# HGRN2 level products in blocks of 32 keys on four column tiles

## The chip, the cores and the metric

The kernel runs on one core of a Trainium2 chip. The metric is device time in microseconds of one execution, as the median over runs. The engines are named as in the profile: PE is TensorE's matmul and PEld its weight load, DVE is VectorE, ACT is ScalarE, POOL is GpSimd, SP is SyncE. L979 is line 979 of the kernel before.

## The reference

A hybrid decoder layer on 2048 tokens of width 1024 in float32. After an RMSNorm and one input projection, four HGRN2 heads of width 128 and eight RWKV-7 heads of width 64 run side by side. Their outputs go through an output projection and a ConvFFN. The change touches the HGRN2 heads alone, and in them the attention-like product within a chunk:

```python
b = jnp.cumsum(gb, axis=2)
diff = b[:, :, :, None, :] - b[:, :, None, :, :]
dec = jnp.exp(jnp.where(causal, diff, -jnp.inf))
A = jnp.einsum('bhtk,bhsk,bhtsk->bhts', qb, kb, dec)
o = jnp.einsum('bhts,bhsv->bhtv', A, vb) + jnp.einsum('bhtk,bhkv->bhtv', qb * jnp.exp(b), S)
```

Here gb is log f, and the decay from key s to query t is the product of f over the tokens between them. The state S is carried from chunk to chunk.

## The kernel before

The work has two stages. The first makes the projections, both kinds of heads and most of the output projection; the second is the ConvFFN. In the first stage three generators run in turn: `rw_stream` (RWKV, one unit for four heads on 512 tokens), `hg_stream` (HGRN, one unit for one head on 512 tokens, 16 units in all) and `dense` (projection matmuls, 128x512 each, three for one product of float32 operands that were split into a high and a low part). A round takes one step of `rw_stream` and one of `hg_stream`, and then `fill` adds dense work for 2000 ns of a written cost (`TICK`). This gives the order in which instructions are written; a list scheduler may move an instruction ahead of another on its engine. Each engine then runs its own list in order. Projection products go to the PSUM pair `pj`, RWKV's to `rw`, HGRN's to `hg`, which has two banks.

In `hg_unit` a head's 512 tokens stand along the free dimension, in four blocks of 128, and the 128 channels on the partitions. The decayed product of q and k in a block is built from levels. At the level of m tokens (m = 1, 2, 4, ..., 64), tokens are paired in runs of m. `scaled(l)` makes a tile X that holds k, scaled with the decay up to the end of its run, in each even run, and q, scaled with the decay from the start of its run, in each odd one. The product of the keys of an even run with the queries of the following odd run is then right for that pair of runs. `scaled` also carries the running products Pf and Sf to the next level, on DVE.

`level(lp, off, kt, qt, l)` makes the products of a level for all four blocks (L979). Up to the level of 32 tokens, blocks of 64 keys are used: for each of the eight blocks of 64 tokens, a weight load of 128 channels x 64 keys and a matmul of 32 queries (those of the odd runs), on the column tile at 0 or 64. The diagonal is one such product with all 64 queries and the unscaled q and k. The result stands with keys on PSUM partitions. `take(l, lp, off)` copies the wanted entries into the tile A (128 partitions, 4 blocks, 64 queries) with a predicated copy on DVE (L985), masked by a constant for the level. The diagonal is first written to A by a multiply with a mask (L997). The masks come with the constants, C_LV and C_DG, in the tile `cst`.

One step of the unit does the diagonal and levels 1, 2 and 4 (the diagonal in a bank of its own, l0, the levels in l1); three steps of `scaled` later another does levels 8, 16 and 32. Then ACT copies A into the two diagonal quarters of Af (128 keys x 128 queries a block). The level of 64 tokens follows as a product of 64x64 blocks (L1023) that ACT copies to the upper right quarter of Af. k scaled to the end of the block is transposed (L1021) and copied to KT by ACT, the states are made from it (L1032), and L1041 and L1042 give the output.

Of the kernel before, what the change touches and what calls it, by code (L numbers as in the profile page):

```python
# [7 lines left out]
F32 = mybir.dt.float32  # L8
F32R = mybir.dt.float32r
BF16 = mybir.dt.bfloat16  # L10
U32 = mybir.dt.uint32
AF = mybir.ActivationFunctionType
# [6 lines left out]
P = 128  # L19
# [10 lines left out]

C_CEN, C_ONE, C_S1, C_DG = 0, 128, 256, 384
C_LV = 448
C_SCAN = C_LV + 6 * 64
C_PAR = C_SCAN + 512
C_ID = C_PAR + 2
C_W = C_ID + 128
# [2 lines left out]
def make_consts():  # L39
    import numpy as np  # L40

    c = np.zeros((P, C_W), np.float32)
    p = np.arange(P)[:, None]
    q = np.arange(P)[None, :]
    same = ((p // 64) == (q // 64)).astype(np.float32)
    c[:, C_ID:C_ID + P] = p == q
    for f in range(2):
        c[:, C_PAR + f] = np.arange(P) % 2 == f
    c[:, C_CEN:C_CEN + P] = (p == q) - same / 64.0
    c[:, C_ONE:C_ONE + P] = same  # L50
    t = np.arange(64)[None, :]
    s = p % 64
    c[:, C_S1:C_S1 + 64] = t > s
    c[:, C_S1 + 64:C_S1 + 128] = t >= s
    c[:, C_DG:C_DG + 64] = t == s
    for l in range(6):
        m = 1 << l
        tq = np.arange(64).reshape(-1, 2, m)[:, 1, :].reshape(1, 32)
        c[:, C_LV + 64 * l:C_LV + 64 * l + 32] = ((tq // (2 * m)) == (s // (2 * m))) & ((s // m) % 2 == 0)
    c[:, C_SCAN:C_SCAN + 512] = (np.arange(512) % 64 != 0)[None, :]  # L60
    return c

# [2 lines left out]
def tile_layer(ctx, tc, consts, x, norm1_w, w_in, hg_lb_logits, hg_norm_w, rw_shift_mu, rw_w0, rw_w2,  # L65
# [4 lines left out]
    V, S, TE = nc.vector, nc.scalar, nc.tensor  # L70
# [13 lines left out]
    cst = cp.tile([P, C_ID], F32, name="cst")  # L84
# [5 lines left out]
    blk1 = cst[:, C_ONE:C_ONE + P]  # L90
    s1m = cst[:, C_S1:C_S1 + P]
    dgm = cst[:, C_DG:C_DG + 64]
    scanm = cst[:, C_SCAN:C_SCAN + 512]

    def pst(name):
# [14 lines left out]
    def act(out_, in_, func, **kw):  # L110

        want = tables.get(func)
        if want is not None and want != tab["now"]:
            pre = S.preload_act_table_set(want)
            for u_ in tab["uses"]:
                tc.add_manual_dep(pre.ins, u_.ins.name, NOSYNC, reason="table order")
            tab.update(now=want, pre=pre, uses=[])
        i_ = S.activation(out_, in_, func, **kw)  # L118
        if want is not None:
            tc.add_manual_dep(i_.ins, tab["pre"].ins.name, NOSYNC, reason="table order")  # L120
            tab["uses"].append(i_)
        return i_
# [12 lines left out]
    off = {}  # L135
    with tc.tile_pool(name="vp", bufs=1, reuse_waits="tile") as vp, tc.tile_pool(name="ps0", bufs=1, space=PSUM, reuse_waits="tile") as pools["ps"]:
        rows = vp.tile([P, P], F32, name="rows")
        V.memset(rows, 0.0)
        n = 0
# [127 lines left out]
    def phase1(c1):  # L267
# [3 lines left out]
        rp = c1.enter_context(tc.tile_pool(name="rp", bufs=1, reuse_waits="tile"))  # L271
# [11 lines left out]
        Af = hp.tile([P, 4, P], F32, name="Af")  # L283
# [6 lines left out]
        def bank(kind):  # L290
            return ps.tile([P, 512], F32, tag=kind, name=kind, bufs=2)
# [18 lines left out]
        def ev_lora(nb):  # L310
            def f(acc):
                t_ = stg("tl", "tl", 1)
                shift_mix(acc, 12, t_)
                act(t_[0:64, :], t_[0:64, :], AF.Tanh)
                stage[("tl", nb)] = t_
            return f
# [192 lines left out]
        def dense():  # L509
# [3 lines left out]
            for nb in range(NBLK):  # L513
                if nb >= 2:
                    jobs.append(("O", nb - 2))
                jobs.append(("A", nb))
                jobs.append(("P", 3584, ev_lora(nb), lambda nb=nb: done["rw1"] >= 2 * nb, None))
# [16 lines left out]

            at = [i for i, jb in enumerate(jobs) if jb[0] == "A"]
            extra = []
# [37 lines left out]
            for n, jb in enumerate(jobs):  # L574
                if jb[0] == "E":
                    jb[1]()
                    continue
                if jb[0] == "A":
                    if jb[1] == 0:
# [28 lines left out]
                acc = bank("pj")  # L608
                then = jobs[n + 1][1] if jobs[n + 1][0] == "A" else None
                for k in range(KD):  # L610
# [322 lines left out]
        def hg_unit(nb, j):  # L933
            q, f, v, gg = (stage.pop((n_, nb, j)) for n_ in "qfvg")
            k = rp.tile([P, BLK], F32, tag="hk", name="hk")
# [5 lines left out]
                TE.transpose(tp[:, b * P:(b + 1) * P], v[:, b * P:(b + 1) * P], ident)  # L941
            act(VT, tp.rearrange("p (b t) -> p b t", t=P), AF.Copy)
            yield
            A = rp.tile([P, 4, 64], F32, tag="hA", name="A")
            Pf = f
            Sf = rp.tile([P, BLK], F32, tag="Sf", name="Sf")
            V.memset(Sf.rearrange("p (n e) -> p n e", e=2)[:, :, 1:2], 1.0)
# [1 line left out]
            def scaled(l):  # L949

                m = 1 << l
                X = rp.tile([P, BLK], F32, tag="hX", name="hX", bufs=3)
                vw = lambda t_: t_.rearrange("p (n e m) -> p n e m", e=2, m=m)
                V.tensor_mul(vw(X)[:, :, 1, :], vw(q)[:, :, 1, :], vw(Pf)[:, :, 1, :])
                n_ = BLK // (2 * m)
                if l == 0:
                    act(vw(X)[:, :, 0, :], vw(k)[:, :, 0, :], AF.Copy)
                    act(vw(Sf)[:, :, 0, :], vw(Pf)[:, :, 1, :], AF.Copy)
                else:
                    V.tensor_mul(vw(X)[:, :, 0, :], vw(k)[:, :, 0, :], vw(Sf)[:, :, 0, :])  # L960
                    V.tensor_mul(vw(Sf)[:, :, 0, :], vw(Sf)[:, :, 0, :],
                                 vw(Pf)[:, :, 1, m - 1:m].broadcast_to([P, n_, m]))
                V.tensor_mul(vw(Pf)[:, :, 1, :], vw(Pf)[:, :, 1, :],
                             vw(Pf)[:, :, 0, m - 1:m].broadcast_to([P, n_, m]))
                return X

            def level(lp, off, kt, qt, l=None):

                w = 64 if l is None else 32
                for b in range(4):  # L970
                    for e in range(2):
                        t0 = (2 * b + e) * 64
                        qs = qt[:, t0:t0 + 64]
                        o = lp[e * 64:e * 64 + 64, off + b * w:off + b * w + w]
                        if l is not None:
                            m = 1 << l
                            qs = qs.rearrange("p (n e m) -> p n e m", e=2, m=m)[:, :, 1, :]
                            o = o.rearrange("p (n m) -> p n m", m=m)
                        TE.matmul(o, kt[:, t0:t0 + 64], qs, start=True, stop=True, tile_position=(0, e * 64))  # L979

            def take(l, lp, off):

                m = 1 << l
                mk = cst[:, C_LV + 64 * l:C_LV + 64 * l + 32].bitcast(U32).rearrange("p (n m) -> p n m", m=m)
                V.copy_predicated(A.rearrange("p b (n e m) -> p b n e m", e=2, m=m)[:, :, :, 1, :],  # L985
                                  mk.unsqueeze(1).broadcast_to([P, 4, 32 // m, m]),
                                  lp[:, off:off + 128].rearrange("p (b n m) -> p b n m", b=4, m=m))

            Xs = []
            for l in range(3):  # L990
                Xs.append(scaled(l))
                yield
            l0, l1 = bank("hg"), bank("hg")
            level(l0, 0, k, q)
            for l in range(3):
                level(l1, l * 128, Xs[l], Xs[l], l)
            V.tensor_mul(A, l0[:, 0:256].rearrange("p (b t) -> p b t", t=64), dgm.unsqueeze(1).broadcast_to([P, 4, 64]))  # L997
            for l in range(3):
                take(l, l1, l * 128)
            yield  # L1000
            Xs = []
            for l in range(3, 6):
                Xs.append(scaled(l))
                yield
            l1 = bank("hg")
            for l in range(3, 6):
                level(l1, (l - 3) * 128, Xs[l - 3], Xs[l - 3], l)
            for l in range(3, 6):
                take(l, l1, (l - 3) * 128)
            act(Af[0:64, :, 0:64], A[0:64], AF.Copy)  # L1010
            act(Af[64:128, :, 64:128], A[64:128], AF.Copy)
            yield
            X = scaled(6)
            V.tensor_mul(k, k, Sf)
# [4 lines left out]
            lp = bank("hg")  # L1019
            for b in range(4):  # L1020
                TE.transpose(tp[:, b * P:(b + 1) * P], k[:, b * P:(b + 1) * P], ident)  # L1021
            for b in range(4):
                TE.matmul(lp[0:64, b * 64:b * 64 + 64], X[:, b * P:b * P + 64], X[:, b * P + 64:b * P + 128],  # L1023
                          start=True, stop=True, tile_position=(0, 0))
# [44 lines left out]
        def hg_stream():  # L1069
            for n in range(4 * NBLK):  # L1070
                while ready["hg"] <= n:
                    yield None
                yield from hg_unit(n // 4, n % 4)
# [47 lines left out]
    with ExitStack() as c2:  # L1121
# [36 lines left out]
        with tc.tile_pool(name="op", bufs=1, reuse_waits="tile") as op_:  # L1158
# [7 lines left out]
            b = NBLK - 1  # L1166
# [41 lines left out]
            def weights(k, dh):  # L1208
                raw = ring("w", w_out[0, k * P:(k + 1) * P, dh * 512:dh * 512 + 512])
                wh, wl = (wo_[c].pop() if wo_[c] else  # L1210
                          op_.tile([P, 512], F32R, tag="wo" + c, name="wo" + c, bufs=3) for c in "hl")
                split_next(wh, wl, raw)
                return wh, wl
# [6 lines left out]
            for dh in range(2):  # L1220
                accs = [pst("wacc") for _ in range(4)]
                for n, k in enumerate((0, 1, 4, 5, 2, 3, 6, 7)):
                    w = weights(k, dh)
                    if dh == 0:
                        take(k)
                    if n == 5:
                        for i in range(4):
                            t0 = b * BLK + i * P
# [10 lines left out]
                    if dh == 1 and 2 <= n:  # L1239
                        for j in range(2):  # L1240
                            q = 2 * (n - 2) + j
# [3 lines left out]
                    for q in range(12):  # L1245
                        i, t_ = (q % 4, q // 4) if first else (q // 3, q % 3)
                        TE.matmul(accs[i], terms[t_][0][:, i * P:(i + 1) * P], terms[t_][1],
                                  start=n == 0 and t_ == 0, stop=n == KD - 1 and t_ == 2)
# [229 lines left out]
    with tc.tile_pool(name="dn", bufs=1, reuse_waits="tile") as dn:  # L1478
# [61 lines left out]
        for s_ in range(DS, N):  # L1540
            g, p, kk = steps[s_]
# [60 lines left out]
```

## Time and profile before

| | |
|---|---|
| median of three runs | 2675.3 us (2671.83 to 2676.13) |
| span of the profiled execution | 2678.7 us; the page gives no other time for it |
| instructions | 47929 |
| PE busy | 2595.9 us (97%) |
| DVE busy | 1964.4 us (73%) |
| ACT busy | 1368.4 us (51%) |
| POOL busy | 383.2 us (14%) |
| DMA | 510.54 MB, mean 191 GB/s |

An engine's busy time is the time in which at least one of its instructions was under way, so instructions that overlap count once; the mean ns of one is its own duration. Shapes of a matmul are given as rows*columns of the array that it uses, and then the partitions and elements of the moving operand. A row of waits reads: who waited, on what, for how many us in total, how often, and the longest.

### The profile page before, as it was taken

The page shows a single profiled execution, that of the slowest core. Times are in us where ns is not written, and L with a number is a line of the kernel's source. Part 1 is how long each engine was busy: PE and PEld are TensorE (multiplying, and loading weights), DVE is VectorE, ACT ScalarE, POOL GpSimd, SP SyncE. Part 2 cuts the span into 40 slices and gives each one's busy share as a digit, 9 for nine tenths or more (in the row PEclk, how much of TensorE's full clock was granted, in tenths as well). Part 3 has the DMA queues.
Part 4 walks back from the last instruction along what each step waited for, and adds up shares of the span by engine and source line. Part 5 has one row for each costly group of instructions (what it writes and reads, how often), then busy time and mean ns, then how long its engine had stood idle before and what let it go on. Part 6 is the DMA issues. An engine that isn't in the chain of part 4 may idle for free. (4 is left out here: it accounts for less than half of the span.)

```text
span 2678.7 us, 47929 instructions
## 1 busy us (share of the span) xinstructions
PE 2595.9 (97%) x18059; PEld 2089.1 (78%) x18059; DVE 1964.4 (73%) x3744; ACT 1368.4 (51%) x2200; POOL 383.2 (14%) x686
## 2 busy tenths in 40 slices
PE   7999999999999999999999999999999999999998
PEld 5877777777777777778778888887888888888887
DVE  4877767676567675667678789988998888676556
ACT  4556453554545455344457655456555545545444
POOL 6433222212222123222100000000000000000000
PEclk9999999999999999999999999999999999999999
DMA  8654443355643546844584458756754463898665
GB/s 301 202 164 165 163 142 116 115 162 183 201 152 115 153 157 221 277 131 129 172 287 139 138 188 262 239 172 194 260 199 150 149 203 124 318 322 280 204 193 185
DMA packets 312702, 510.54 MB, mean 191 GB/s; under 512 B 46879, under 2 KB 143509, under 8 KB 312469
## 3 DMA queue, kind: packets, MB, share of 16 engines
q1 hardware_dynamic: 257937, 329.13, 37.3%
q0 software_dynamic: 54464, 178.32, 20.4%
q8 instruction: 142, 2.33, 0.4%
q14 instruction: 91, 0.75, 0.1%
q10 hardware_dynamic: 68, 0.02, 0.0%
HBM read 373.13 MB, written 134.22 MB: 189 GB/s over the span
## 5 line engine op out<-in xcount | busy, mean ns | idle before, releaser
L263 PE MATMUL pj<-hh,wh 128*128 128x512 f32 x960 | 394.1, 411 | 6.7 <-ACT rkv L118 1.6
L264 PE MATMUL pj<-hl,wh 128*128 128x512 f32 x960 | 377.9, 394 | 0.0
L265 PE MATMUL pj<-hh,wl 128*128 128x512 f32 x960 | 377.7, 394 | 0.0
L263 PE MATMUL ua<-Bh,uwh 128*128 128x512 f32 x704 | 276.1, 392 | 3.8 <-ACT m L118 2.6
L265 PE MATMUL ua<-Bh,uwl 128*128 128x512 f32 x704 | 274.3, 390 | 0.0
L264 PE MATMUL ua<-Bl,uwh 128*128 128x512 f32 x704 | 274.1, 389 | 0.0
L263 PEld LDWEIGHTS pj<-hh,wh 128*128 128x128 f32 x960 | 181.1, 189 | 56.6 <-issue 9.1
L265 PEld LDWEIGHTS pj<-hh,wl 128*128 128x128 f32 x960 | 181.0, 189 | 39.6 <-issue 0.2
L264 PEld LDWEIGHTS pj<-hl,wh 128*128 128x128 f32 x960 | 181.3, 189 | 34.3 <-issue 0.6
L247 ACT CAST uwh<-uraw 128x512 fp32r<-128x512 f32 x220 | 135.2, 618 | 137.7 <-PE ua L264 63.3
L248 DVE TENSOR_TENSOR dal<-draw,dah 128x512 fp32r<-128x512 f32 x138 | 95.3, 690 | 111.3 <-ACT dah L247 110.0
L248 DVE TENSOR_TENSOR uwl<-uraw,uwh 128x512 fp32r<-128x512 f32 x220 | 147.5, 687 | 35.0 <-ACT uwh L247 34.9
L247 ACT CAST dah<-draw 128x512 fp32r<-128x512 f32 x138 | 85.9, 622 | 163.7 <-PE da L264 79.1
L263 PEld LDWEIGHTS ua<-Bh,uwh 128*128 128x128 f32 x704 | 132.1, 188 | 33.2 <-ACT m L118 4.8
L265 PEld LDWEIGHTS ua<-Bh,uwl 128*128 128x128 f32 x704 | 132.2, 188 | 28.1 <-DVE uwl L248 0.4
L264 PEld LDWEIGHTS ua<-Bl,uwh 128*128 128x128 f32 x704 | 132.2, 188 | 26.8
L263 PE MATMUL ud<-Bh,uwh 128*128 128x512 f32 x352 | 138.0, 392 | 0.0
L265 PE MATMUL ud<-Bh,uwl 128*128 128x512 f32 x352 | 137.0, 389 | 0.0
L264 PE MATMUL ud<-Bl,uwh 128*128 128x512 f32 x352 | 137.0, 389 | 0.0
L1472 POOL DMA_DIRECT2D gd<-y x2 | 1.1, 542 | 945.3 <-DVE y L1470 945.3
L264 PE MATMUL da<-dbl,dah 128*128 128x512 f32 x332 | 129.4, 390 | 0.3 <-DVE dbl L248 0.2
L265 PE MATMUL da<-dbh,dal 128*128 128x512 f32 x332 | 129.2, 389 | 0.0
(580 smaller groups left out, 6268.9 us busy)
## 6 DMA issues: line engine op xcount, KB each, us to landing
uraw<-in_w_up_dram SPq DMA_DIRECT2D x176, 256.0 KB, 3.3
woraw<-in_w_out_dram POOLq DMA_DIRECT2D x96, 256.0 KB, 3.4
br<-gd SPq DMA_DIRECT2D x88, 256.0 KB, 4.0
draw<-Sg SPq DMA_DIRECT2D x88, 256.0 KB, 2.8
draw<-Tw SPq DMA_DIRECT2D x88, 256.0 KB, 3.1
gd<-y SPq DMA_DIRECT2D x86, 256.0 KB, 2.8
Sg<-br SPq DMA_DIRECT2D x72, 256.0 KB, 2.1
xt<-x1d SPq DMA_DIRECT2D x32, 512.0 KB, 6.1
```

The lines of the kernel that those rows point to most:

```text
L247: S.copy(hi, src)
L248: V.tensor_sub(lo, src, hi.bitcast(F32))
L263: TE.matmul(acc, lh, rh, start=first, stop=False, skip_group_check=skip)
L264: TE.matmul(acc, lh, rl, start=False, stop=False, skip_group_check=skip)
L265: TE.matmul(acc, ll, rh, start=False, stop=last, skip_group_check=skip)
L1472: (dma if end is None else nc.gpsimd.dma_start)(gd_[2 * h + b][fb * P:(fb + 1) * P, :], ys[0][:, b * BLK:(b + 1) * BLK])
```

## The change

Up to the level of 16 tokens the keys are taken in blocks of 32 on the four column tiles at 0, 32, 64 and 96: 16 products of 32 keys by 16 queries a level, and 16 of 32 by 32 for the diagonal. The level of 32 tokens is made as `across` does it: in each of the eight blocks of 64 tokens the first 32 tokens as keys and the last 32 as queries, on the column tiles at 0 and 64, with no mask, and ACT copies the result from PSUM straight to its place in Af. A shrinks to 32 queries a block, and the masks with it. The diagonal goes into the same bank as levels 1, 2 and 4. ACT copies A to Af in four pieces of 32 partitions instead of two of 64.

```diff
 C_LV = 448
-C_SCAN = C_LV + 6 * 64
+C_D32 = C_LV + 5 * 16
+C_SCAN = C_D32 + 32
...
-            A = rp.tile([P, 4, 64], F32, tag="hA", name="A")
+            A = rp.tile([P, 4, 32], F32, tag="hA", name="A")
...
-                w = 64 if l is None else 32
+                w = 32 if l is None else 16
                 for b in range(4):
-                    for e in range(2):
-                        t0 = (2 * b + e) * 64
-                        qs = qt[:, t0:t0 + 64]
-                        o = lp[e * 64:e * 64 + 64, off + b * w:off + b * w + w]
+                    for c0 in range(0, P, 32):
+                        t0 = b * P + c0
+                        qs = qt[:, t0:t0 + 32]
+                        o = lp[c0:c0 + 32, off + b * w:off + b * w + w]
                         if l is not None:
                             m = 1 << l
                             qs = qs.rearrange("p (n e m) -> p n e m", e=2, m=m)[:, :, 1, :]
                             o = o.rearrange("p (n m) -> p n m", m=m)
-                        TE.matmul(o, kt[:, t0:t0 + 64], qs, start=True, stop=True, tile_position=(0, e * 64))
+                        TE.matmul(o, kt[:, t0:t0 + 32], qs, start=True, stop=True, tile_position=(0, c0))
+
+            def across(lp, off, X):
+
+                for b in range(4):
+                    for c0 in (0, 64):
+                        t0 = b * P + c0
+                        TE.matmul(lp[c0:c0 + 32, off + b * 32:off + b * 32 + 32], X[:, t0:t0 + 32],
+                                  X[:, t0 + 32:t0 + 64], start=True, stop=True, tile_position=(0, c0))
...
                 V.copy_predicated(A.rearrange("p b (n e m) -> p b n e m", e=2, m=m)[:, :, :, 1, :],
-                                  mk.unsqueeze(1).broadcast_to([P, 4, 32 // m, m]),
-                                  lp[:, off:off + 128].rearrange("p (b n m) -> p b n m", b=4, m=m))
+                                  mk.unsqueeze(1).broadcast_to([P, 4, 16 // m, m]),
+                                  lp[:, off:off + 64].rearrange("p (b n m) -> p b n m", b=4, m=m))
...
-            l0, l1 = bank("hg"), bank("hg")
-            level(l0, 0, k, q)
+            l1 = bank("hg")
+            level(l1, 192, k, q)
             for l in range(3):
-                level(l1, l * 128, Xs[l], Xs[l], l)
-            V.tensor_mul(A, l0[:, 0:256].rearrange("p (b t) -> p b t", t=64), dgm.unsqueeze(1).broadcast_to([P, 4, 64]))
+                level(l1, l * 64, Xs[l], Xs[l], l)
+            V.tensor_mul(A, l1[:, 192:320].rearrange("p (b t) -> p b t", t=32), dg32.unsqueeze(1).broadcast_to([P, 4, 32]))
             for l in range(3):
-                take(l, l1, l * 128)
+                take(l, l1, l * 64)
...
-            for l in range(3, 6):
-                level(l1, (l - 3) * 128, Xs[l - 3], Xs[l - 3], l)
-            for l in range(3, 6):
-                take(l, l1, (l - 3) * 128)
-            act(Af[0:64, :, 0:64], A[0:64], AF.Copy)
-            act(Af[64:128, :, 64:128], A[64:128], AF.Copy)
+            for l in range(3, 5):
+                level(l1, (l - 3) * 64, Xs[l - 3], Xs[l - 3], l)
+            across(l1, 128, Xs[2])
+            for l in range(3, 5):
+                take(l, l1, (l - 3) * 64)
+            for c0 in (0, 64):
+                act(Af[c0:c0 + 32, :, c0 + 32:c0 + 64],
+                    l1[c0:c0 + 32, 128:256].rearrange("p (b t) -> p b t", t=32), AF.Copy)
+            for c0 in range(0, P, 32):
+                act(Af[c0:c0 + 32, :, c0:c0 + 32], A[c0:c0 + 32], AF.Copy)
```

More of the change, by code (lines that the diff above doesn't have):

```diff
@@ L55, in make_consts @@
     c[:, C_DG:C_DG + 64] = t == s
-    for l in range(6):
+    s = p % 32
+    for l in range(5):
         m = 1 << l
-        tq = np.arange(64).reshape(-1, 2, m)[:, 1, :].reshape(1, 32)
-        c[:, C_LV + 64 * l:C_LV + 64 * l + 32] = ((tq // (2 * m)) == (s // (2 * m))) & ((s // m) % 2 == 0)
+        tq = np.arange(32).reshape(-1, 2, m)[:, 1, :].reshape(1, 16)
+        c[:, C_LV + 16 * l:C_LV + 16 * l + 16] = ((tq // (2 * m)) == (s // (2 * m))) & ((s // m) % 2 == 0)
+    c[:, C_D32:C_D32 + 32] = np.arange(32)[None, :] == s
     c[:, C_SCAN:C_SCAN + 512] = (np.arange(512) % 64 != 0)[None, :]
@@ L92, in tile_layer @@
     dgm = cst[:, C_DG:C_DG + 64]
+    dg32 = cst[:, C_D32:C_D32 + 32]
     scanm = cst[:, C_SCAN:C_SCAN + 512]
@@ L978, in level @@
                             o = o.rearrange("p (n m) -> p n m", m=m)
-                        TE.matmul(o, kt[:, t0:t0 + 64], qs, start=True, stop=True, tile_position=(0, e * 64))
+                        TE.matmul(o, kt[:, t0:t0 + 32], qs, start=True, stop=True, tile_position=(0, c0))
[5 more added lines that the diff above has]
+                                  X[:, t0 + 32:t0 + 64], start=True, stop=True, tile_position=(0, c0))
             def take(l, lp, off):
                 m = 1 << l
-                mk = cst[:, C_LV + 64 * l:C_LV + 64 * l + 32].bitcast(U32).rearrange("p (n m) -> p n m", m=m)
+                mk = cst[:, C_LV + 16 * l:C_LV + 16 * l + 16].bitcast(U32).rearrange("p (n m) -> p n m", m=m)
                 V.copy_predicated(A.rearrange("p b (n e m) -> p b n e m", e=2, m=m)[:, :, :, 1, :],
-                                  mk.unsqueeze(1).broadcast_to([P, 4, 32 // m, m]),
-                                  lp[:, off:off + 128].rearrange("p (b n m) -> p b n m", b=4, m=m))
+                                  mk.unsqueeze(1).broadcast_to([P, 4, 16 // m, m]),
+                                  lp[:, off:off + 64].rearrange("p (b n m) -> p b n m", b=4, m=m))
             Xs = []
```

## Prediction, made before the changed kernel ran

> **What bounds the kernel now.** I read the page's span and engine totals first, then the stretches on either side of the end of the first stage, then the first stage's waits of TensorE, then the rows of the products themselves.
>
> ```profile
> span 2678.7 us, 47929 instructions
> ...
> PE 2595.9 (97%) x18059; PEld 2089.1 (78%) x18059; DVE 1964.4 (73%) x3744; ACT 1368.4 (51%) x2200; POOL 383.2 (14%) x686
> ```
>
> The stretches (us, then busy time of each engine, granted clock, DMA share, GB/s):
>
> ```profile
> 0.00:1330.26 1330.26, 1267.04 (x12208) 998.27 (x12208) 898.38 (x2136) 648.81 (x1043) 364.33 (x652) 0.99 0.53 171
> 1330.26:2678.70 1348.44, 1328.86 (x5853) 1090.81 (x5851) 1065.99 (x1609) 719.54 (x1157) 18.83 (x35) 1.00 0.64 210
> ```
>
> TensorE is busy 97% of the span, and 1267.04 of 1330.26 us in the first stage, where the change lies. There it idles 63.2 us; VectorE is busy 68% of that stretch, ScalarE 49%. So TensorE's own instruction stream is the bound, and time taken out of it shortens the stage unless it turns into waiting. Its longest waits there:
>
> ```profile
> PE vps L152 <- DMA cst<-in_consts_dram: 11.3, 1, 11.3
> PE rw L857 <- ACT M L118: 10.1, 7, 2.2
> ...
> PE hg L1021 <- DVE hk L1014: 3.4, 1, 3.4
> ...
> PE hg L1032 <- ACT KT L118: 0.8, 2, 0.4
> ```
>
> The largest is the start of the kernel. Only the last two belong to HGRN's chain, and they occur three times. In none of these rows does TensorE wait for what `take` leaves in A.
>
> **The products before.** Two bursts of one HGRN unit, from the timeline of TensorE (start us, us, what), and the groups by shape (rows*columns of the array, moving shape; busy us, mean ns of one):
>
> ```profile
> 398.85 0.69 PE L979 MATMUL hg<-hq,hk 128*64 128x64 f32 x16
> 399.37 1.54 PE L979 MATMUL hg<-hX 128*64 128x32 f32 x48
> 400.84 0.50 PE L263 MATMUL pj<-hh,wh 128*128 128x512 f32 x1
> ...
> 409.22 1.59 PE L979 MATMUL hg<-hX 128*64 128x32 f32 x48
> 410.75 0.50 PE L263 MATMUL pj<-hh,wh 128*128 128x512 f32 x1
> ```
>
> ```profile
> L979 PE MATMUL hg<-hX 128*64 128x32 f32 x1536 | 52.2, 223 | 0.0
> L979 PE MATMUL hg<-hq,hk 128*64 128x64 f32 x256 | 11.9, 229 | 0.0
> L811 PE MATMUL rw<-TZ,M 32*32 32x32 f32 x512 | 6.0, 193 | 0.6 <-DVE TZ L798 0.5
> ```
>
> The code writes 16 units x 6 levels x 8 = 768 level products and the row counts 1536, so each float32 product is two instructions. From its first start to the next projection matmul the first burst holds TensorE 1.99 us, the second 1.53 us: 3.52 us a unit, 56.3 us over 16 units. The pace inside the second is (1.59 - 0.223) / 47 = 29.1 ns an instruction. These alternate between two column tiles, so one tile is held 58 ns. The moving operand is 64 columns wide in the diagonal's products and 32 in the others. The first burst holds 16 instructions more than the second for 1.99 - 1.53 = 0.46 us, again 29 ns each, although those move twice as much: the moving width does not set the pace.
>
> Does a tile of 32 columns turn faster, and do four run together? No row has 128 rows on 32 columns. The two nearest are of RWKV:
>
> ```profile
> 428.38 0.75 PE L811 MATMUL rw<-TZ,M 32*32 32x32 f32 x64
> 429.07 0.50 PE L263 MATMUL pj<-hh,wh 128*128 128x512 f32 x1
> ...
> 596.94 0.69 PE L871 MATMUL rw<-M 64*64 64x64 f32 x32
> ```
>
> L871 uses four tiles of 64 rows by 64 columns in turn. With about 0.23 us for one (as in the 64-column rows above), (0.69 - 0.23) / 31 = 14.8 ns an instruction, 59 ns a tile. That is the 58 ns of 128 rows by 64 columns: halving the rows does not change a tile's turn. L811 goes round four tiles, one in each group of 32 columns: (0.75 - 0.193) / 63 = 8.8 ns, 35 ns a tile. Columns halve it. After the last start TensorE needs 0.69 - 63 x 0.0088 = 0.13 us more.
>
> **The change, part by part.** (1) Levels of 1 to 16 tokens and the diagonal. Today a unit's first burst has 8 + 3 x 8 products, 64 instructions. It gets 16 + 3 x 16, 128 instructions on four column tiles. The known ends for their pace are 8.8 ns (L811) and 14.6 ns (a tile keeps its 58 ns, four of them run together). I take 8.8, since the turn followed the columns and not the rows in the three rows above: 127 x 0.0088 + 0.13 = 1.25 us instead of 1.99.
>
> (2) The second burst: 2 x 16 products on four tiles, 64 instructions, and the level of 32 tokens as 8 products on two tiles, 16 instructions at half the rate (17.6 ns): 63 x 0.0088 + 16 x 0.0176 + 0.13 = 0.97 us instead of 1.53.
>
> Together 2.22 us for 3.52: 1.30 us a unit, 20.8 us over 16 units. Each burst is entered from and left to 128-column matmuls as before, so those turns stay, being inside the starts used.
>
> Here the Trainium skill speaks against the change. TensorEngine Tiling (Array Packing), section Instruction Overhead, gives each matmul about 60 cycles of overhead and advises against taking the tiling factor from a dimension that is already small; moving operands of 32 become 16. TensorE: Matmul & The Clock Gate, section Back-to-back issue gap, puts those 60 cycles at about 25 ns. By that 208 instructions would take 5.2 us a unit instead of 2.22, and the change would lose about 27 us, as an estimate from these pages. The trace does not bear it out as a pace of the whole array: L811 moves 32 columns at 8.8 ns an instruction.
>
> (3) VectorE. One multiply of 256 elements becomes one of 128; six predicated copies of 128 become five of 64.
>
> ```profile
> L985 DVE COPY_PREDICATED A<-cst,hg 128x128 f32<-128x128 uint32 x96 | 32.8, 342 | 5.0 <-PE hg L979 4.8
> L997 DVE TENSOR_TENSOR A<-hg,cst 128x256 f32<-128x256 f32 x16 | 6.8, 422 | 2.9 <-PE hg L979 2.7
> L794 DVE TENSOR_TENSOR Ti<-Ti,etmp 128x128 f32<-128x128 f32 x8 | 2.3, 286 | 0.0
> ```
>
> Before: 422 + 6 x 342 = 2474 ns. From 256 to 128 elements a tensor operation drops 136 ns, 1.06 ns an element, so 64 fewer give 342 - 68 = 274: after, 286 + 5 x 274 = 1656 ns. That is 0.82 us a unit and 13 us of VectorE's 898. I cost it at nothing: VectorE is not the bound. One wait is added. The diagonal now shares a PSUM bank with three levels, so its multiply waits for the whole first burst, where today it runs beside the levels. Behind it on VectorE are the `take`s and the `scaled` of the next levels. It ends at 1.25 + 0.29 = 1.54 us after the burst's start, and the `take`s cannot start today before 1.99: no loss.
>
> (4) ScalarE. Two copies of A on 64 partitions x 256 become four of 32 x 128, and two of the same size come from PSUM.
>
> ```profile
> L118 ACT ACTIVATE Af<-A 64x256 f32<-64x256 f32 x32 | 13.2, 414 | 19.1 <-DVE A L985 18.8
> L118 ACT ACTIVATE Af<-hg 64x256 f32<-64x256 f32 x16 | 6.0, 376 | 0.5 <-PE hg L1023 0.4
> L240 ACT CAST hh<-oraw 128x256 fp32r<-128x256 f32 x8 | 3.2, 404 | 6.8 <-DMA oraw<-oT 6.8
> L495 ACT CAST group<-cst 128x128 fp32r<-128x128 f32 x1 | 0.3, 296 | 0.0
> ```
>
> 128 elements fewer save 404 - 296 = 108 ns. So 4 x (414 - 108) + 2 x (376 - 108) = 1760 ns instead of 828: 0.93 us more a unit, 15 us on ScalarE's 649. Hidden where TensorE has projection matmuls. Queued behind on ScalarE are the projection evictions and the copy to KT, for which L1032 waits. The `take`s end about 0.4 us sooner after the second burst and the burst 0.56 us, so KT comes about when it came, but TensorE arrives sooner.
>
> (5) What is given back. Where TensorE already waits in HGRN's chain after a burst (three times: L1032 twice, L1021 once), the saving of that unit becomes waiting; with one more such unit that is 4 x 0.7 = 2.8 us, taking the second burst's share and a little of ScalarE's. Ends: nothing, or all 1.30 us in half the units, 10.4 us. Below nothing too: L857's wait and others fed by VectorE could shrink by some of the 13 us taken off it; I allow 6 us.
>
> (6) Banks asked of the `hg` pair fall from nine to eight a unit, and the constants' load is 272 columns (139 KB) shorter; no wait in the rows above hangs on either, both at nothing.
>
> Sum: 2678.7 - 20.8 + 2.8 = 2660.7 us of span for the profiled execution. The page gives no time for it but the span, and that stands 3.4 us above the median of the runs, 2675.3. The change of -18 us on the median gives 2657 us.
>
> **The rivals.** No gain from narrow tiles: the 58 ns stays with a tile, or four tiles of 128 rows do not run at once. Then a unit takes 192 x 14.6 + 16 x 29.1 ns = 3.27 us and two tails of 0.13 = 3.53, against 3.52: nothing, 2675 us, or up to 3 more with the give-back of (5). Against it stands L811's 35 ns; for it, that L811 has 32 rows and also splits them over two row groups.
>
> Waiting takes the gain: the 10.4 us of (5) and more such places in RWKV's chain (L857, 7 waits), where a shorter burst covers less of ScalarE's work. With 15 us given back, 2669 us. Against it: the whole list of waits behind the start is short.
>
> Slower, by the supply of instructions.
>
> ```profile
> q8 instruction: 142, 2.33, 0.4%
> ```
>
> 2.33 MB in 142 packets is 16.4 KB each. The 18059 matmuls and as many weight loads are 36118 instructions, 65 bytes each if that queue is TensorE's, so a packet holds about 254. The first burst, 256 instructions with its weight loads, uses one up in 1.25 us; today half of one in 1.99. A packet takes about 0.004 x 16 x 2678.7 / 142 = 1.2 us. If the stream waits one packet in each of 32 bursts, 38.6 us come on top: 2657 + 39 = 2696 us. It decides from 0.56 us a burst (18 / 32). Against it: L811's 64 products ran at 8.8 ns without a break, but that is half a packet.
>
> Slower, by a pace of 29 ns for every instruction whatever its tile: 208 x 29.1 ns = 6.05 us for 3.26, 45 us more, 2720 us. L871 and L811 speak against it. The skill's pages above belong to this case.
>
> **How the numbers follow.** Forecast 0.78, no gain 0.08, waiting takes the gain 0.07, supply 0.05, pace 0.02. A measurement of this kernel tells about 0.2%, 5.4 us, from no change. Faster: 0.78 and most of the waiting case, 0.84; same: no gain and little else, 0.09; slower: 0.07. The forecast's own range is 2648 (20.8 + 6 saved) to 2665 (10.4 given back). For 8 in 10 I reach to the waiting case: 2648 to 2669.
>
> **What would show it.** The new product groups at 128*32 with 3072 and 256 instructions, a burst of 128 held about 1.25 us to the next start, the second about 0.97. Predicated copies near 274 ns, copies to Af near 300. The stage's TensorE busy time about 20 us less, its second stage unchanged. I am wrong if the bursts pace at 14 ns or more, if gaps appear inside them, or if the bursts shrink and the stage's idle time grows beyond 63 us by as much.

## The result, and the profile after

The changed kernel takes 2662.4 us (median; 2661.71 to 2663.6), before 2674.47: ratio 0.9948, interval 0.9931 to 0.9965. A second set of rounds gave 2662.79 against 2675.33, ratio 0.9946 (0.9929 to 0.9963). The change makes the kernel about 13 us faster, by its interval between 9 and 19 us. The forecast was 18 us.

First the stretches of both kernels, cut at the first matmul of the second stage (the prediction cut the kernel before at 1330.26 us, 15 us ahead of it). The columns are us, busy time of PE, PEld, DVE, ACT and POOL, clock, DMA share and GB/s; two lines of the kernel before, then two of the changed one.

```profile
0.00:1345.40 1345.40, 1280.47 (x12258) 1007.32 (x12258) 907.55 (x2148) 660.48 (x1061) 368.01 (x658) 0.99 0.52 171
1345.40:2678.70 1333.30, 1315.42 (x5803) 1081.77 (x5801) 1056.82 (x1597) 707.87 (x1139) 15.15 (x28) 1.00 0.64 211
```

```profile
0.00:1324.03 1324.03, 1257.48 (x13794) 986.01 (x13795) 893.62 (x2132) 674.22 (x1123) 366.10 (x657) 0.99 0.53 173
1324.03:2661.80 1337.77, 1317.55 (x5803) 1081.96 (x5801) 1056.54 (x1597) 708.64 (x1142) 15.81 (x29) 1.00 0.63 210
```

The first stage ends 21.4 us sooner. TensorE is busy 23.0 us less in it and idles 66.5 us instead of 64.9. VectorE is busy 13.9 us less and ScalarE 13.7 us more. The second stage, whose code is unchanged, is 4.5 us longer. So the span falls 16.9 us.

The bursts of one unit, from the timeline of TensorE in the changed kernel, and its groups by shape (busy us, mean ns):

```profile
109.66 0.46 PE L983 MATMUL hg<-hq,hk 128*32 128x32 f32 x32
109.94 1.03 PE L983 MATMUL hg<-hX 128*32 128x16 f32 x96
110.90 0.50 PE L267 MATMUL pj<-hh,wh 128*128 128x512 f32 x1
...
119.98 0.72 PE L983 MATMUL hg<-hX 128*32 128x16 f32 x63
120.53 0.21 PE L990 MATMUL hg<-hX 128*32 128x32 f32 x1
120.54 0.18 PE L983 MATMUL hg<-hX 128*32 128x16 f32 x1
120.55 0.43 PE L990 MATMUL hg<-hX 128*32 128x32 f32 x15
120.91 0.50 PE L267 MATMUL pj<-hh,wh 128*128 128x512 f32 x1
```

```profile
L983 PE MATMUL hg<-hX 128*32 128x16 f32 x2560 | 30.0, 186 | 0.8 <-issue 0.6
L983 PE MATMUL hg<-hq,hk 128*32 128x32 f32 x512 | 8.0, 202 | 0.8 <-DVE hk L940 0.8
L990 PE MATMUL hg<-hX 128*32 128x32 f32 x256 | 7.2, 198 | 0.0
```

The first burst holds TensorE 110.90 - 109.66 = 1.24 us where it held 1.99, the second 120.91 - 119.98 = 0.93 where it held 1.53. That is 1.35 us a unit, 21.6 us over 16 units if every burst ran like these. Some are drawn out: over the whole trace, from each burst's start to the next start of other work, the sums are 58.2 us before and 37.7 us after, 20.5 us.

VectorE and ScalarE, the groups by shape:

```profile
L997 DVE COPY_PREDICATED A<-cst,hg 128x64 f32<-128x64 uint32 x80 | 20.2, 252 | 0.2
L1009 DVE TENSOR_TENSOR A<-hg,cst 128x128 f32<-128x128 f32 x16 | 4.5, 283 | 0.0
```

```profile
L122 ACT ACTIVATE Af<-A 32x128 f32<-32x128 f32 x64 | 19.7, 308 | 0.9
L122 ACT ACTIVATE Af<-hg 32x128 f32<-32x128 f32 x32 | 8.5, 265 | 26.3 <-DVE A L997 19.5 <-DVE etmp L796 3.6 <-PE pj L268 3.0
```

And TensorE's waits up to 1400 us (total us, times, longest), one line of the kernel before, then four of the changed one:

```profile
PE pj L263 <- ACT hh L240: 5.6, 8, 1.1
```

```profile
PE pj L267 <- ACT hh L244: 9.5, 10, 3.4
...
PE hg L1037 <- DVE hk L1030: 4.3, 2, 3.6
...
PE wacc L1263 <- DVE Bl L245: 1.4, 1, 1.4
...
PE hg L983 <- issue: 0.6, 2, 0.3
```

The wait for the split of a product's input into its high and low part (hh) was 5.6 us in 8 waits, none over 1.1 us; its longest is now 3.4 us, near 1288 us. The wait for Bl, at the first products of the second stage, is for the low part of the last heads' outputs. It did not occur before.

### The profile page after: what moved, and what is told of

It reads as the page before. It is cut to its first block, busy times and chain, and to the rows that moved or that the text cites. A ratio compares the mean times of both kernels' runs of the same rounds, so it can differ in the third digit from the quotient of the medians.

```text
span 2661.8 us, 51045 instructions
## 1 busy us (share of the span) xinstructions
PE 2575.0 (97%) x19595; PEld 2068.0 (78%) x19595; DVE 1950.2 (73%) x3728; ACT 1382.9 (52%) x2264; POOL 381.9 (14%) x686
## 4 chain that ended last, share of the span: by engine, by line
PE 66%; DVE 13%; DMA 9%; ACT 7%; issue 3%; SPq 0%; POOL 0%; DVEq 0%; ACTq 0%; POOLq 0%
PE pj L267 7%; PE pj L268 6%; PE pj L269 6%; PE ua L267 4%; PE ua L269 4%; PE ua L268 4%; PE da L268 2%; PE da L269 2%; PE da L267 2%; PE ud L269 2%; PE ud L268 2%; PE ud L267 2%; PE db L268 2%; PE db L267 2%; PE db L269 2%
```

## The experiments

**Both kernels once more.** No edit.

> The kernel before, unchanged, profiled once more. In the first pair of profiles the span fell 16.9 us (2678.7 to 2661.8), the medians 12.1 us, and the products' bursts alone 20.6 us. Theory 1 (the profile of before was a slow execution): a second profile has a span near 2672.5, with the start of the first matmul of the last output projection near 1339 us instead of 1345.4, and the ratio to before is 1.000 within 0.002. Theory 2 (executions repeat, and the medians differ from the profiles for a reason that is in the kernel): a span near 2678.7 again.

Measured: 2677.87 us, ratio 1.001 (0.9997 to 1.0023), span 2683.0, first matmul of the second stage at 1348.0 us. The first profile of before was no exception; theory 1 falls. Executions of one kernel scatter over some 15 us (before: 2668.08 to 2682.36 in the 29 runs beside these), so single spans do not settle a few microseconds.

> The changed kernel, unchanged, in five rounds, to set the size of the gain and to repeat its profile. If all of the bursts' 20.6 us arrives, the ratio is 0.9923; if the 18 us of the prediction, 0.9933; if 12 us as in the first medians, 0.9955.

Measured: ratio 0.9946 (0.9929 to 0.9963). The interval holds the 18 us of the prediction (0.9933) and the 12 us of the first medians (0.9955), and not all of the bursts' 20.6 (0.9923). Its stretches and its wait at the hand-over:

```profile
0.00:1322.91 1322.91, 1255.80 (x13794) 983.89 (x13795) 893.39 (x2132) 673.96 (x1123) 365.59 (x657) 0.99 0.53 173
1322.91:2661.50 1338.59, 1317.60 (x5803) 1082.78 (x5801) 1056.94 (x1597) 707.62 (x1142) 15.81 (x29) 1.00 0.63 210
```

```profile
PE wacc L1263 <- DVE Bl L245: 3.4, 1, 3.4
```

Again the first stage is short and the second long. Over three profiles with the products of before (the two of before and the next experiment) the second stretch took 1333.1 to 1335.0 us, over two of the changed kernel 1337.8 and 1338.6: in these profiles 3 to 5 us are given back there.

**ScalarE's part alone.**

```diff
-            act(Af[0:64, :, 0:64], A[0:64], AF.Copy)
-            act(Af[64:128, :, 64:128], A[64:128], AF.Copy)
+            for c0 in (0, 64):
+                act(Af[c0:c0 + 32, :, c0 + 32:c0 + 64], A[c0:c0 + 32, :, 32:64], AF.Copy)
+            for c0 in range(0, P, 32):
+                act(Af[c0:c0 + 32, :, c0:c0 + 32], A[c0:c0 + 32, :, c0 % 64:c0 % 64 + 32], AF.Copy)
```

> The kernel before with only ScalarE's part of the change: the copies of A to its two quarters of Af are made in six pieces of 32 partitions x 128 elements instead of two of 64 x 256 (some 0.9 us more ScalarE a unit, 15 us in all). The products stay on 64-column tiles. Theory 1 (the missing part of the gain is lost behind these copies): 4 to 9 us slower than before, ratio 1.0015 to 1.0035, and TensorE's waits on KT grow from 0.8 us. Theory 2 (the copies are hidden, and the missing part comes from elsewhere): within 2 us of before.

Measured: 2675.95 us, ratio 1.000 (0.9989 to 1.0011). The copies cost nothing that these runs resolve:

```profile
L118 ACT ACTIVATE Af<-A 32x128 f32<-32x128 f32 x96 | 29.3, 307 | 21.5 <-DVE A L985 20.6
```

ScalarE does 29.3 us in place of 13.2, and TensorE's wait on KT stays at 0.8 us.

**The copies on VectorE.** `act(Af[...], A[...], AF.Copy)` in the loop over four pieces became `V.tensor_copy(Af[...], A[...])`.

> The changed kernel with the four copies of A to Af on VectorE instead of ScalarE: about 1.2 us less ScalarE and 0.8 us more VectorE a unit, so that VectorE is back near its load of before. Theory 1 (the missing gain is lost behind ScalarE's copies): 3 to 8 us faster than the changed kernel, about 2656 us. Theory 2 (copies hidden): within 2 us of the changed kernel, 2660 to 2664 us.

Measured: 2672.64 us, ratio 0.9989 (0.9978 to 1.000): 10 us slower than the changed kernel. Neither theory had that. The group by shape and TensorE's longest wait:

```profile
L1027 DVE COPY Af<-A 32x128 f32<-32x128 f32 x64 | 14.0, 219 | 0.9
```

```profile
PE hg L1037 <- DVE hk L1030: 13.0, 7, 7.9
```

With 14 us more on VectorE most of the gain is gone; some 4 of the 10 us go with a lower granted clock (median 0.9925 for 0.994, at the 2.4 us for each 0.001 worked out below). k times Sf (L1030), which TensorE needs for its transposes, comes right after the copies in VectorE's order, and TensorE waits 13.0 us for it instead of 4.3. Whether the copies alone or also the new order made it was not separated. For this chain the way over ScalarE, beside VectorE, is the cheaper one.

**All blocks on one tile before the next.**

```diff
-                for b in range(4):
-                    for c0 in range(0, P, 32):
+                for c0 in range(0, P, 32):
+                    for b in range(4):
```

> The changed kernel with two loops of level exchanged: all four blocks of 128 tokens on one column tile, then the next tile, so that eight instructions in a row go to the same tile of 32 columns. The same products, the same number of instructions. Theory 1 (a tile of 32 columns is held 35 ns and four of them run at once): eight in a row take about 7 x 35 + 9 = 254 ns, a burst of 128 instructions 4.1 us instead of 1.24 and the second 2.4 instead of 0.93, so about 4.4 us a unit and 70 us in all more than the changed kernel, about 2732 us. Theory 2 (8.9 ns is the pace of issue for narrow products, whichever tile they go to): no change, 2660 to 2666 us.

Measured: 2694.45 us, ratio 1.0069 (1.0047 to 1.009), 32 us more than the changed kernel: neither 0 nor 70. One first burst in the timeline, its start and the next start:

```profile
110.34 0.80 PE L983 MATMUL hg<-hq,hk 128*32 128x32 f32 x29
...
113.00 0.50 PE L267 MATMUL pj<-hh,wh 128*128 128x512 f32 x1
```

It takes 2.66 us, 20 ns an instruction. So going round the four tiles is what gives 8.9 ns, and theory 2 falls. But one tile does not hold up the next as far as I had thought. Read in the written order, the eight starts on the first tile lie, after a first step of 53, about 32 ns apart (at 0, 53, 84, 116, 148, 179, 211 and 243 ns), and the second tile's begin at 154 ns, between them: as if two tiles were served at a time. The trace names no tile for a start, so this reading is not shown beyond its times. The bursts' sum rose from 37.7 to 70.7 us, 33.0, and the time by 31.7: TensorE's time in the bursts passes to the end nearly in full in this run.

**The level of 64 tokens on two column tiles.**

```diff
-                TE.matmul(lp[0:64, b * 64:b * 64 + 64], X[:, b * P:b * P + 64], X[:, b * P + 64:b * P + 128],
-                          start=True, stop=True, tile_position=(0, 0))
+                c0 = 64 * (b % 2)
+                TE.matmul(lp[c0:c0 + 64, b // 2 * 64:b // 2 * 64 + 64], X[:, b * P:b * P + 64],
+                          X[:, b * P + 64:b * P + 128], start=True, stop=True, tile_position=(0, c0))
```

ScalarE copies the result in two pieces instead of one.

> The changed kernel with the level of 64 tokens on two column tiles of 64 in turn instead of on one: blocks 1 and 3 on the tile at 64, and ScalarE copies the result in two pieces of 64 x 128 (268 ns each) instead of one of 64 x 256 (376). Theory 1 (a tile of 64 columns is held 58 ns, two run at once, and freed TensorE time in the first stage arrives): 8 instructions take about 0.23 us instead of 0.47, 0.24 us a unit, 3.7 us faster than the changed kernel, about 2659 us. Theory 2 (small gains of this size are lost in the order that the scheduler makes anew): anything from 5 us faster to 5 us slower.

Measured: 2663.48 us, ratio 0.9957 (0.9941 to 0.9974): the same as the changed kernel. The group fell about as forecast, from 11.2 us in the changed kernel (11.5 before) to 7.8:

```profile
L1040 PE MATMUL hg<-hX 128*64 128x64 f32 x128 | 7.8, 240 | 0.0
```

TensorE idled in its first stage 69.4 us instead of 66.5 and 67.1. A gain of this size can be lost in waits, and it is below what the rounds resolve. This version does not beat the changed kernel. Its second stretch took 1334.6 us with a wait of 2.6 us for Bl, so the 3 to 5 us of the two profiles above are no fixed price of the narrow products.

**Every narrow product twice.** `for _ in range(2):` before the matmul of `level`.

> The changed kernel with every product of the diagonal and of the levels of 1 to 16 tokens issued twice (the level of 32 once): 192 instructions a unit more at 8.8 ns, 1.7 us a unit, 27 us of TensorE in all, at the same place. Theory 1 (TensorE's time in these bursts passes to the end in full): 27 us slower than the changed kernel, about 2690 us. Theory 2 (a part of the bursts' time is covered by waits that stay, as 14 of 20.6 us would say): some 18 us slower, about 2681 us.

Measured: 2749.47 us, ratio 1.0269 (1.0244 to 1.0294), 87 us more than the changed kernel, three to five times what the theories said. A first burst, with 512 instructions, in the timeline, between two projection matmuls of the same kind ahead of it and behind it, and the wait:

```profile
109.25 0.39 PE L268 MATMUL pj<-hl,wh 128*128 128x512 f32 x1
...
110.46 1.42 PE L984 MATMUL hg<-hX 128*32 128x16 f32 x131
114.45 0.84 PE L984 MATMUL hg<-hX 128*32 128x16 f32 x58 [2.58 <-issue]
...
115.82 0.63 PE L268 MATMUL pj<-hl,wh 128*128 128x512 f32 x1
```

```profile
PE hg L984 <- issue: 36.9, 16, 4.7
```

In the middle of nearly every first burst TensorE stands still, for nothing that the profile names. The instruction packets around this burst started at 105.77 us (1.0 us long) and 111.52 us (1.6 us), each 16384 bytes. The queue's rows of the changed and of the doubled kernel:

```profile
q8 instruction: 154, 2.52, 0.4%
```

```profile
q8 instruction: 178, 2.92, 0.5%
```

From before to the changed kernel (142 to 154 packets) 1536 matmuls and as many weight loads were added, and from there to the doubled kernel 3072 of each: 256 TensorE instructions a packet both times. So the queue is TensorE's. The second packet was there at 113.09 us, though, and TensorE went on at 114.45: the traces do not show what filled the time between.

The granted clock fell too (0.986 for 0.994 of before and after). Behind the gap it stands at 0.50 from 115.00 to 118.41 us, and the projection matmul there takes 0.63 us instead of 0.39. Over the spans the missing clock is (1 - 0.986) x 2746.2 = 38 us against (1 - 0.994) x 2661.8 = 16. So, as an estimate, 27 us of products, 36 of gaps and 22 of clock make 85 of the 87 us. This run says nothing clean of TensorE's time, but it shows TensorE stalling in bursts one doubling above the change, as the rival of the supply has it.

**The doubled products, in two bursts.** Against the doubled kernel:

```diff
-            for l in range(3):
+            level(l1, 0, Xs[0], Xs[0], 0)
+            yield
+            for l in range(1, 3):
                 level(l1, l * 64, Xs[l], Xs[l], l)
```

> The kernel with the doubled products, with one more step between the diagonal with level 1 and levels 2 and 4, so that about 2 us of dense work stand between two bursts of 128 instructions where the doubled kernel has one burst of 256 (512 with their weight loads). The same products as the doubled kernel, which took 2749 us, 86 us more than the changed kernel: TensorE idled 40 us inside its first bursts, for nothing that the profile names but issue, some 2.5 us in each. Theory 1 (instructions come in packets of 16.4 KB, some 256 instructions, that take 1.0 to 1.6 us each, and a burst of 512 uses two of them up faster than the next one comes): idle time inside the bursts falls from 40 us to under 5, and the time to about 2692 us, the changed kernel's and 27 us. Theory 2 (the second product into the same PSUM place is held up, or ScalarE and VectorE cannot follow): the gaps stay, 2740 us or more.

Measured: 2729.38 us, ratio 1.0197 (1.0176 to 1.0219). The wait, and one unit's first two bursts:

```profile
PE hg L984 <- issue: 9.2, 7, 3.2
```

```profile
773.29 0.76 PE L984 MATMUL hg<-hq,hk 128*32 128x32 f32 x58
...
774.67 0.50 PE L267 MATMUL pj<-hh,wh 128*128 128x512 f32 x1
...
776.91 1.43 PE L984 MATMUL hg<-hX 128*32 128x16 f32 x128
778.70 0.50 PE L267 MATMUL pj<-hh,wh 128*128 128x512 f32 x1 [0.36 <-DVE Ti L798]
```

With the same products the gaps fall from 36.9 to 9.2 us. So the length of the burst makes most of them, and not the second write to a place; under 5 us, as theory 1 had it, they did not come. That TensorE waits for the packets of instructions fits both runs, but no run changed the packets alone. The time missed its 2692 by 37 us. Some 14 of them go with the clock (0.989 of 2727.3 us, 30 us missing against 16) and 9 with the gaps that are left. The added step also puts 2 us more dense work into each unit, which was not tried alone.

**The dense work between steps.** In the changed kernel, `TICK = 2000.0` became 1900.0, and 2100.0.

> The changed kernel with 1900 instead of 2000 ns of dense work written between two steps, so that more dense work is left for the end of the first stage. Both profiles of the changed kernel show TensorE waiting 3.1 to 3.4 us for a split of the attention output near 1288 us and 1.4 to 3.4 us at the first matmuls after the stage, and neither profile of before shows the second. Theory 1 (TensorE runs out of covering work at the end of the stage): these waits shrink and the kernel gains 2 to 5 us, about 2659 us. Theory 2 (the waits hang on the chain alone): they stay, and the time is within 3 us or worse, since less work covers each step.

Measured: 2669.83 us, ratio 0.9977 (0.9964 to 0.999), 7 us slower than the changed kernel. The wait for Bl at the first matmuls of the second stage is gone, the longest for hh stays at 3.1 us, and the first stage grew to 1332.7 us. Half of theory 1 holds, without its gain.

> The changed kernel with 2100 instead of 2000 ns of dense work written between two steps. With 1900 the wait at the hand-over to the second stage went, but the first stage grew by 9 us. Theory 1 (each step has less cover now that the bursts are 1.3 us a unit shorter, and more dense work between steps gives it back): 2 to 5 us faster than the changed kernel, about 2659 us. Theory 2 (the dense work is then used up before the chains end, and the end of the stage waits): 3 us slower or more, with a first matmul of the second stage that comes later than 1324 us.

Measured: 2693.38 us, ratio 1.0071 (1.0044 to 1.0098), 31 us slower, as theory 2 had it. TensorE's longest wait:

```profile
PE pj L267 <- ACT hh L244: 14.7, 11, 5.4
```

The first matmul of the second stage comes at 1350.0 us. But the place is not the one of theory 2: 11.6 of the 14.7 us lie between 100 and 1250 us, and projection matmuls still run at 1342 us, so the dense work is not used up early. The clock, 0.988, goes with about half of the loss (32 us missing against 16). Why the split of hh comes late in this order stays open. 2000 is the best of the three.

## Why the prediction was right, and what it got wrong

The bursts came out as worked: 1.25 and 0.97 us forecast, 1.24 and 0.93 in the timeline; 20.8 us forecast for all units, 20.5 measured in the first pair of profiles and 19.6 (58.9 to 39.3) in the second. The pace of L811, four tiles of 32 columns, carried over to 128 rows (the no-gain rival falls). By L811 the 25 ns an instruction of the Trainium skill (TensorE: Matmul & The Clock Gate, Back-to-back issue gap) were set aside; at 8.9 ns in the changed kernel, (1.24 - 0.11) / 127 with 0.11 us after the last start, with 16 columns moving, the trace now contradicts them for products on different column tiles.

The predicated copy was put at 274 ns and took 252, the multiply 286 and 283; the copies to Af 306 and 268 and took 308 and 265. Both engines' shifts (13 us less, 15 more; 13.9 and 13.7 measured in the first stage) cost or gave nothing, as assumed. The run with ScalarE's part alone shows that for ScalarE; for VectorE no run does.

The mechanism held; the term that was mis-sized is the give-back (5): 2.8 us forecast, at L1021 and L1032. These two waits grew from 3.4 and 0.8 to 4.3 and 1.3, 1.4 us. In the two profiles of the changed kernel more was given back at a place that the prediction did not name, the hand-over to the second stage. In both profiles of before the gate product of the last RWKV unit starts 9.5 us ahead of the second stage (1335.89 and 1345.40), in both of the changed kernel 7.6 us, so less work stands there to cover store, load and split of the last heads' outputs. The kernel before, then the changed one:

```profile
1335.89 1.88 PE L925 MATMUL rw<-gdt,g 128*128 128x512 f32 x4
...
1345.40 1.08 PE L1247 MATMUL wacc<-woh,Bh 128*128 128x512 f32 x4
```

```profile
1316.40 1.98 PE L929 MATMUL rw<-gdt,g 128*128 128x512 f32 x4 [0.48 <-ACT yo L122]
...
1324.03 1.09 PE L1263 MATMUL wacc<-woh,Bh 128*128 128x512 f32 x4
```

The second stage then takes 3 to 5 us longer. The new wait of 1.4 and 3.4 us is part of it; about 2 us of the rest are busy time of TensorE, which no run here explains. That the wait goes with 1900 ns fits the cover, but one run with another order does not prove it. The run with two tiles for the level of 64 speaks against it as the whole cause: it has the same 7.6 us and the wait, and no longer second stage.

The spans fell by 16.9 and 21.5 us (first and second pair), the medians by 12 to 13. A part of this difference goes with the granted clock, which the prediction did not weigh. In the 58 executions of the kernel before beside the experiments the mean time falls from 2682.9 us at a clock of 0.992 to 2668.8 at 0.998, about 2.4 us for each 0.001. Their median clock is 0.995; the changed kernel's ten executions have 0.992 to 0.995, mostly 0.993 and 0.994. At the same 0.994 the means are 2678.2 us (7 executions) and 2663.2 (4), 15 us apart. So some 3 us of the missing gain go with a lower clock. Whether the longer waits lower it was not tested. What is left lies within the interval of the second measurement, which holds the ratio forecast, 0.9933.

The supply rival did not decide, but the stalls that it foresaw came at twice the burst's length. The bursts of 256 instructions stood still for 0.6 us in all in the first profile and 1.4 in the second, against the 18 us (0.56 us a burst) from which it would have decided. The forecast was 2657 us, 2648 to 2669; measured were 2662.4 and 2662.8.

## What to carry to other kernels

Narrow products paid here because they go round the column tiles: read the turn of a tile and the number of tiles from a row of the trace that uses such tiles, and divide the turn by the number. Then look where the saved time meets the end of a stage, where the covering work may have shrunk with it; compare runs at the same granted clock before explaining a few microseconds; and price what moves by the engine that the chain waits on: 15 us more on ScalarE cost nothing here, and moving the copies to VectorE lost 10 us. Long bursts of very short instructions can stall with nothing to wait for in the profile, as the 512 here did; count them with their weight loads.

## What the hardware showed that was not expected

A burst of 512 short TensorE instructions (256 matmuls at about 9 ns with their weight loads) stalled for 2.58 us in the case shown (36.9 us in 16 waits over the kernel). Bursts of 256 hardly stalled in the changed kernel (0.6 and 1.4 us in all, 3.5 with 2100 ns of dense work), but for 9.2 us where two of them followed each other with about 2 us of dense work between. Behind the stall shown, the granted clock stood at 0.50 for 3.4 us, so a stall can cost more than its own length. Not every gap has such a stretch behind it: none follows the gap of 2.18 us at 296.04 us in the changed kernel. Eight instructions in a row on one column tile of 32 columns run at 20 ns each and not at the 32 to 35 ns of a tile's turn. By their times, instructions of the next tile start while the tile before still has some to do.
